# Order of splits, loads and sums around the output projections of a sparse-attention block

## Chip, cores and metric

The kernel runs on one core of a Trainium2 chip. Its time is the device time of one execution in microseconds (us). The engines are TensorE (PE), VectorE (DVE), ScalarE (ACT), GpSimd (POOL) and SyncE (SP); SP, ACT and POOL also issue DMAs, each from its own queue in order.

## The reference, cut to what matters

One block of a decoder trunk: 512 tokens of width 2048, a mixer of native sparse attention (compressed, selected and window branches, 16 heads), then a SwiGLU feed-forward layer of width 5632, then a last normalization. With these sizes only the attention mixer is used.

```python
def rmsnorm(x, g):
    x32 = x.astype(jnp.float32)
    y = x32 * lax.rsqrt(jnp.mean(x32 * x32, axis=-1, keepdims=True) + RMS_EPS)
    return (y * g.astype(jnp.float32)).astype(x.dtype)

def swiglu(h, w_in, w_out):
    z = h @ w_in
    a, b = z[..., :D_FF], z[..., D_FF:]
    return (jax.nn.silu(a) * b) @ w_out

def reference(x, ...):
    h = x
    for i in range(DEPTH):
        hn = rmsnorm(h, mix_norm_g[i])
...
        h = h + nsa_mixer(hn, ...)
...
        h = h + swiglu(rmsnorm(h, ffn_norm_g[i]), ffn_w_in[i], ffn_w_out[i])
    return rmsnorm(h, final_norm_g)
```

## The kernel before

Every matrix product is made of three matmuls in a 32-bit format of lower precision: each operand is split into a high part (an ACT copy into that format) and a low part (a DVE subtraction), and `three` (L275) multiplies high by high, high by low and low by high into the same bank. So every weight costs an ACT and a DVE instruction before PE can use it. `Weights` (L61) loads pieces of 128 x 1024 into three `raw` buffers from SP's queue, splits them into four `whi`/`wlo` buffers, and `take` hands out the next piece, with so many more split ahead. The order of the instructions on each engine is the order in which the code writes them.

**The stages.** The attention mixer comes first (to about 717 us). Along with it the first 1536 columns of the output projection are computed for the first 12 heads, added to `x`, and spilled to `d_h`.

The output projection (L885 to L954) holds the running sum `acc`, four tiles of 128 tokens by 2048 columns. L891 loads columns 1536 on of `x` into it and L892, on POOL's queue, the 1536 spilled columns of all four tiles in one DMA. Then a pass over the last columns, and a loop over tiles `t` and column blocks `cb`: matmuls of the last four heads into one of four banks `po[cb]`, `add` (DVE), a square with a running sum (ACT, L943) whose output goes to a throwaway tile of the four `pp` banks, and for `t` over 0 the transposes of the tile before (`turned`), which need two `pp` banks each. `scaled` applies the norm of the tile, and the finished `acc` rows go to `d_r`.

The first feed-forward product follows (to about 1653 us), in units `q`, with a seven-product scheme for 2 x 2 blocks (Strassen's kind): `split_unit`, `products` and `merge`. Its results go to `d_a`, one slab per pair of inner chunks `j`.

The second product (L1225 to L1433) runs over four column blocks `b` and, in each, 22 units `j` in the order of `ORDER[b]`; `seq` numbers all 88 of them `n`. A unit is either one of seven products (`seven_unit`, 42 matmuls of 256 columns; the inner chunks in `SEVEN[b]`) or plain (`plain_tile` for four token tiles, 24 matmuls of 512 columns). For units of the seven kind the input sums are formed from `d_a` in `form`, and kept in SBUF (`KEPT`, five `asl` slots) or stored in `d_s` and loaded again by `load_seven`, through two `ast` slots. Inputs of plain units, called held, are loaded by `load_a` into one of two places (`rawx`, `tt`) and split by `split_a` into `thi`/`tlo`; `tt` is also where `weight_sums` puts the sums of a seven-kind weight. The residual `acc` is read back from `d_r` by `load_residual` on POOL's queue: columns 0 to 1024 at the start (L1321), the rest as `form` releases the columns that it uses as scratch. At the end of the seven kind's units in a block, `merge_sums` adds the four shared banks `qs` into `acc`; it is written into the next unit, after that unit's splits. `ready` squares a finished block and multiplies it by the last norm's weight.

The last four units of the last block, all plain, form the tail (L1414 to L1435): tile by tile, so that a tile can be finished while the next one is multiplied. A tile's finish is `add`, the square, the multiplication by the weight, `rstd` (sum, mean, root on ACT, and one Newton step on DVE) and four scalings with their stores. `ffn_banks` gives four banks of eight, `po` and `qs` one set each.

Of the kernel before, what the change touches and what calls it, by code (L numbers as in the profile page):

```python
# [10 lines left out]
F32 = mybir.dt.float32  # L11
# [169 lines left out]
def nsa_block(ctx: ExitStack, tc: tile.TileContext, x, rel_bias, mix_g, ffn_g, fin_g, w_in, w_out,  # L181
# [707 lines left out]
    acc = accp.tile([128, NT, D], F32, name="acc")  # L889
    spill = 256 * N_SPILL  # L890
    nc.sync.dma_start(acc[:, :, spill:], x[:, spill:].rearrange("(t p) c -> p t c", p=128))  # L891
    pool.dma_start(acc[:, :, :spill], d_h.rearrange("(t p) c -> p t c", p=128))  # L892

    def add(t, cb, p):
        a = acc[:, t, 512 * cb:512 * (cb + 1)]
        dve.tensor_tensor(a, a, p, op=OP.add)
# [13 lines left out]
    with tc.tile_pool(name="n2", bufs=1) as n2:  # L910
        act(warm, epsc, AF.Sqrt)
        gb2 = n2.tile([128, D], F32, name="gb2")
        pool.dma_start(gb2, ffn_g[0:1, :].to_broadcast([128, D]))
        xn = n2.tile([128, D + 64], F32, name="xn")
        wr_h = n2.tile([128, 7, 1024], F32R, name="wr_h")
        wr_l = n2.tile([128, 7, 1024], F32R, name="wr_l")
        for i in range(7):
            W.place[marks[0] + i] = wr_h[:, i], wr_l[:, i]
        for cb in range(N_SPILL // 2, 4):
            po = out_tiles()  # L920
            for i in range(6):
                w = W.take(2 if cb < 3 else min(2 + i, 6))
                for t in range(NT):
                    tokmajor(po[t], w, heads(i), i == 0, i == 5, t)
            W.ahead(3)
            for t in range(NT):
                add(t, cb, po[t])
        w8 = []
        for t in range(NT):
            ss = smallp.tile([128, 4], F32, name="ss4")  # L930
            po = out_tiles()
            for cb in range(4):
                for i in range(2):
                    if t == 0:
                        w8.append(W.take(7 - len(w8)))
                    tokmajor(po[cb], w8[2 * cb + i], heads(6 + i), i == 0, i == 1, t)
                add(t, cb, po[cb])
                if cb == 3:
                    pool.dma_start(d_r[t], acc[:, t])
                if t and cb in (1, 2):  # L940
                    turned(xn, (2 * cb - 2, 2 * cb - 1), t - 1)
                junk = ps3.tile([128, 512], F32, name="pp")
                act(junk, acc[:, t, 512 * cb:512 * (cb + 1)], AF.Square, accum_out=ss[:, cb:cb + 1])  # L943
            scaled(acc[:, t], rstd(ss), gb2, xn)
            W.ahead((0, 1, 3, 3)[t])
        pa = [ps3.tile([128, 512], F32, name="pp") for _ in range(2)]
        gs = []
        for i in range(4):
            gs.append(W.take(min(2, 3 - i)))
            run(ws(pa, i, gs[i], 0, 256, of=n2_hl))  # L950
            if i in (1, 2):
                turned(xn, (2 * i - 2, 2 * i - 1), 3)
        act(warm, epsc, AF.Silu)
# [152 lines left out]
    def merge(p):  # L1106

        A, B, C, F = banks.pop(p)
        p += N_PLAIN
        e = E[p] = ep.tile([128, 6, 256], F32, name="E")  # L1110

        def both(x):
            return x.unsqueeze(1).to_broadcast([128, 2, 256])

        act(e[:, 1], A[:, 0], AF.Copy)
        plus(e[:, 0:5:4], both(e[:, 1]), B)
        plus(e[:, 5], e[:, 4], F[:, 0])
        plus(e[:, 1], e[:, 5], A[:, 1])
        plus(e[:, 2:4], e[:, 4:6], both(C[:, 0]))
        plus(e[:, 2], e[:, 2], C[:, 1])  # L1120
        if p % 2:
            dve.tensor_tensor(gate_out(p), gate_out(p), gate_out(p - 1), op=OP.mult)
            keep_a(p)
        else:
            act(gate_out(p), gate_out(p), AF.Silu)
# [44 lines left out]


    held, free = {}, {"rawx": -1, "tt": -1}
    for n, (b, j) in enumerate(seq):
        home = "tt"
        if j not in SEVEN[b]:
            home = min(free, key=free.get)
            held[n] = home, free[home]
        free[home] = n

    def load_a(m):  # L1180

        for n, (home, after) in held.items():
            if after == m:
                t = tp.tile([128, 1024 if home == "rawx" else 1536], F32, name=home, bufs=1)
                a_raw[n] = t[:, :2 * S]
                nc.sync.dma_start(a_raw[n], d_a[seq[n][1]])

    def split_a(n):
        if n in held:
            if n >= NU - N_TAIL:  # L1190
                h, l = (asl.tile([128, 1792], F32R, name=f"a{x}")[:, 48:48 + 2 * S] for x in "hl")
            else:
                h, l = (tp.tile([128, 1600], F32R, name=f"t{x}")[:, :2 * S] for x in ("hi", "lo"))
            act(h, a_raw[n], AF.Copy)
            sub(l, a_raw.pop(n), f32(h))
            a_hl[n] = h, l
        elif n < NU:
            a_hl[n] = seven[seq[n][1]] if seq[n][1] in KEPT else passing.pop(0)
        load_a(n)

    t_hl = {}

# [26 lines left out]
    for q in range(NQ):  # L1229
        if q + 1 < NQ:  # L1230
            split_unit(q + 1)
        else:
            W2.ahead(1)
            load_a(-1)
            split_a(0)
        if q + 3 < NQ:
            load_unit(q + 3)
        if q and q % 2 == 0:
            merge(q // 2 - 1)
        products(q)  # L1240
    merge(NQ // 2 - 1)
    front.close()

# [4 lines left out]
    asl = ctx.enter_context(tc.tile_pool(name="asl", bufs=len(KEPT)))  # L1248
    ast = ctx.enter_context(tc.tile_pool(name="ast", bufs=2))
    late2 = ctx.enter_context(tc.tile_pool(name="late2", bufs=1))  # L1250
    ss = [late2.tile([128, 4], F32, name=f"sf{t}") for t in range(NT)]
    n_visit = [0]
    scratch = [acc[:, :, 1024:1536], acc[:, :, 1536:]]
    forms = [n for n, (b, j) in enumerate(seq) if j in SEVEN[b] and (not b or j not in SEVEN[b - 1])]
# [5 lines left out]
    def load_residual(c):  # L1260
        pool.dma_start(acc[:, :, c], d_r[:, :, c].rearrange("t p c -> p t c"))
# [56 lines left out]
            keep_seven(seq[v][1], h, l)  # L1318
            n_visit[0] += 1

    load_residual(slice(0, 1024))  # L1321
    load_form(0)
    load_form(1)
    forming = {n: form(i) for i, n in enumerate(forms)}
# [48 lines left out]
            yield  # L1373

    w8, todo = [], iter(())
    n, na, pending = 0, 1, None
    for b in range(4):
        units = ORDER[b][:-N_TAIL] if b == 3 else ORDER[b]
        po = ffn_banks()
        qs = dict(zip(("p1", "p5", "p6", "p7"), ffn_banks()))  # L1380
        first7 = next(j for j in units if j in SEVEN[b])
        last7 = [j for j in units if j in SEVEN[b]][-1]
        started = False
        for i, j in enumerate(units):
            left = len(units) - 1 - i if b == 3 else 9
            w = W2.take(max(1, 3 - left))
            while na <= n + 1 + max(0, 2 - left):
                split_a(na)
                na += 1
            if pending is not None:  # L1390
                merge_sums(*pending)
                pending = None
            for k in (1, 2, 3, 4):
                next(forming.get(n + k, iter(())), None)
            if j in SEVEN[b]:
                seven_unit(n, w, first7)
            else:
                for t in range(NT):
                    plain_tile(n, w, t, not started, b < 3 and i == len(units) - 1)
            started = True  # L1400
            if j == last7:
                pending = b, qs
            load_seven(n)
            if i >= 4:
                next(todo, None)
            if i == 12:
                gf = late2.tile([128, 512], F32, name="gf")
                nc.sync.dma_start(gf, fin_g[None, 512 * b:512 * (b + 1)].to_broadcast([128, 512]))
            n += 1
        if b < 3:  # L1410
            for t in range(NT):
                add(t, b, po[t])
            todo = ready(b, gf)
    c = slice(1536, 2048)  # L1414
    act(warm, epsc, AF.Sqrt)
    for t in range(NT):
        for i in range(N_TAIL):
            if t == 0:
                w8.append(W2.take(N_TAIL - 1 - i))
                if na < NU:  # L1420
                    split_a(na)
                    na += 1
            plain_tile(n + i, w8[i], t, False, i == N_TAIL - 1)
        add(t, 3, po[t])
        act(po[t], acc[:, t, c], AF.Square, accum_out=ss[t][:, 3:4])
        dve.tensor_tensor(acc[:, t, c], acc[:, t, c], gf, op=OP.mult)
        y = rstd(ss[t])
        for cb in range(4):
            c4 = slice(512 * cb, 512 * (cb + 1))
            src = acc[:, t, c4]  # L1430
            if cb % 2:
                act(src, src, AF.Copy, scale=y)
            else:  # L1433
                dve.tensor_scalar(src, src, y, None, op0=OP.mult)
            (nc.scalar if cb % 2 else nc.sync).dma_start(out[tok(t), c4], src)  # L1435


_INS = ["x", "rel_bias", "mix_norm_g", "ffn_norm_g", "final_norm_g", "nsa_w_in", "nsa_w_out",
# [25 lines left out]
```

## Time and profile before

| | us |
|---|---|
| median of 3 runs | 2132.6 |
| lowest and highest | 2127.05 and 2134.82 |
| the profiled execution | 2126.48 |
| its span in the trace | 2124.5 |
| DVE busy | 1581.9 |
| ACT busy | 998.3 |

In the trace an instruction has its start from the beginning of the span, its duration, its engine, the line of the kernel and the tiles that it writes and reads. A bracket behind it tells how long its engine was idle ahead of it and what it waited for. Matmuls overlap, so that the distance between the starts of two of them says more than their durations. The granted clock is TensorE's, as a share of full speed. PEld is PE's loading of stationary operands; SPq, ACTq and POOLq are the issues of DMAs.

### The profile page before, as it was taken

Reading aid. Unit: us, or ns where it says so; the run is one execution under the profiler, and the core shown is the slowest. Engines: PE = TensorE matmul, PEld = TensorE weight load, DVE = VectorE, ACT = ScalarE, POOL = GpSimd, SP = SyncE. Lnnn points to the kernel's source line nnn. Section 1 sums busy time; section 2 is a strip of 40 time slices with the busy share of each in tenths; the row PEclk is TensorE's granted clock in tenths of the full one; section 3 lists DMA queues with packets and bytes.
Section 4 is the critical chain, followed back from the end, with each engine's and each line's share of the span. In section 5 each row is a group of like instructions: output and inputs, shape, how many; then the busy total and the mean of one; then the engine's idle time right before and its main releaser. Section 6 shows DMA issues by size and latency. Waiting matters only on the chain.

```text
span 2124.5 us, 37555 instructions
## 1 busy us (share of the span) xinstructions
PE 2101.5 (99%) x14831; PEld 1955.1 (92%) x14831; DVE 1581.9 (74%) x2586; ACT 998.3 (47%) x1625; POOL 145.4 (7%) x234
## 2 busy tenths in 40 slices
PE   9999999999999999999999999999999999999997
PEld 7888898888999978999999999999999888999996
DVE  5565667666666366988888888888887778786775
ACT  5344676666655333444343443434433544444444
POOL 2000111111111100000000000000000000000000
PEclk9999999999999999999999999999999999999998
DMA  6655577766796743444343443334333876878784
GB/s 202 187 157 164 157 203 196 194 184 190 225 296 207 233 168 100 137 131 130 120 126 123 130 126 124 121 123 135 120 128 108 312 265 221 320 262 315 272 306 149
DMA packets 257313, 391.26 MB, mean 184 GB/s; under 512 B 27466, under 2 KB 183162, under 8 KB 256496
## 3 DMA queue, kind: packets, MB, share of 16 engines
q1 hardware_dynamic: 227472, 263.64, 39.9%
q0 software_dynamic: 27936, 122.07, 17.1%
q10 hardware_dynamic: 1728, 3.15, 0.4%
q8 instruction: 116, 1.90, 0.4%
q14 instruction: 61, 0.50, 0.1%
HBM read 323.15 MB, written 70.88 MB: 185 GB/s over the span
## 4 chain that ended last, share of the span: by engine, by line
PE 92%; DMA 4%; DVE 2%; ACT 1%; issue 1%; POOL 0%; ACTq 0%; SPq 0%; POOLq 0%; DVEq 0%
PE f L277 14%; PE f L278 13%; PE f L276 13%; PE proj L278 13%; PE proj L276 13%; PE proj L277 13%; PE pp L277 1%; PE pp L278 1%; PE pp L276 1%; DMA pt<-d_p 1%; PE o L277 1%; PE s L276 1%; PE o L278 1%; PE s L278 1%; PE s L277 1%; PE o L276 1%
## 5 line engine op out<-in xcount | busy, mean ns | idle before, releaser
L97 DVE TENSOR_TENSOR wlo<-raw,whi 128x1024 fp32r<-128x1024 f32 (+1 forms) x225 | 270.6, 1206 | 80.6 <-ACT whi L94 80.3
L94 ACT ACTIVATE whi<-raw 128x1024 fp32r<-128x1024 f32 (+1 forms) x225 | 233.2, 1040 | 194.5 <-DVE raw L969 123.5
L276 PE MATMUL proj<-hn_h,whi 128*128 128x512 f32 (+1 forms) x840 | 293.9, 350 | 2.0 <-ACT whi L94 2.0
L278 PE MATMUL proj<-hn_h,wlo 128*128 128x512 f32 (+1 forms) x840 | 291.2, 347 | 0.5 <-DVE wlo L97 0.5
L277 PE MATMUL proj<-hn_l,whi 128*128 128x512 f32 (+1 forms) x840 | 291.0, 346 | 0.0
L969 DVE TENSOR_TENSOR tlo<-tt,thi 128x1536 fp32r<-128x1536 f32 (+2 forms) x134 | 196.0, 1462 | 109.3 <-ACT thi L1071 86.7
L1066 ACT ACTIVATE whi<-raw 128x1024 fp32r<-128x1024 f32 x123 | 126.1, 1058 | 293.7 <-DVE raw L969 290.3
L278 PE MATMUL f<-hn_h,wlo 128*128 128x256 f32 x656 | 181.1, 276 | 0.0
L276 PE MATMUL f<-hn_h,whi 128*128 128x256 f32 x656 | 181.1, 276 | 0.0
L277 PE MATMUL f<-hn_l,whi 128*128 128x256 f32 x656 | 181.1, 276 | 0.0
L278 PEld LDWEIGHTS proj<-hn_h,wlo 128*128 128x128 f32 x840 | 158.1, 188 | 22.5 <-DVE wlo L97 1.2
L276 PEld LDWEIGHTS proj<-hn_h,whi 128*128 128x128 f32 x840 | 158.3, 188 | 19.4 <-ACT whi L94 2.2
L277 PEld LDWEIGHTS proj<-hn_l,whi 128*128 128x128 f32 x840 | 158.1, 188 | 17.2 <-issue 0.2
L276 PE MATMUL proj<-whi,hn_h 128*128 128x256 f32 (+2 forms) x568 | 162.9, 287 | 0.0
L278 PE MATMUL proj<-whi,hn_l 128*128 128x256 f32 (+2 forms) x568 | 162.4, 286 | 0.0
L277 PE MATMUL proj<-wlo,hn_h 128*128 128x256 f32 (+2 forms) x568 | 162.2, 286 | 0.0
L1071 ACT ACTIVATE thi<-tt 128x1536 fp32r<-128x1536 f32 x82 | 121.8, 1486 | 82.6 <-PE proj L277 82.5
L969 DVE TENSOR_TENSOR wlo<-raw,whi 128x1024 fp32r<-128x1024 f32 x123 | 147.0, 1223 | 1.1 <-ACT whi L1066 1.1
L277 PEld LDWEIGHTS f<-hn_l,whi 128*128 128x128 f32 x656 | 123.2, 188 | 0.0
L276 PEld LDWEIGHTS f<-hn_h,whi 128*128 128x128 f32 x656 | 123.1, 188 | 0.0
L278 PEld LDWEIGHTS f<-hn_h,wlo 128*128 128x128 f32 x656 | 123.1, 188 | 0.0
L760 ACT ACTIVATE p<-p,ms 128x31 f32<-128x31 f32 (+2 forms) x192 | 90.6, 473 | 43.4 <-DVE ms L758 40.6
(346 smaller groups left out, 6232.2 us busy)
## 6 DMA issues: line engine op xcount, KB each, us to landing
raw<-in_ffn_w_in SPq DMA_DIRECT2D x135, 512.0 KB, 3.7
raw<-in_ffn_w_out SPq DMA_DIRECT2D x88, 512.0 KB, 5.8
rawx<-in_ffn_w_in SPq DMA_DIRECT2D x41, 512.0 KB, 4.8
rawx<-d_a SPq DMA_DIRECT2D x34, 512.0 KB, 4.9
ah<-d_s POOLq DMA_DIRECT2D x16, 896.0 KB, 6.9
al<-d_s POOLq DMA_DIRECT2D x16, 896.0 KB, 9.2
raw<-in_nsa_w_in SPq DMA_DIRECT2D x24, 512.0 KB, 4.9
raw<-in_nsa_w_in POOLq DMA_DIRECT2D x24, 512.0 KB, 6.1
```

The costliest lines, as they stand in the source:

```text
L94: self.nc.scalar.activation(hi[:, :n], src, AF.Copy)
L97: self.nc.vector.tensor_tensor(lo[:, :n], src, hi[:, :n].bitcast(F32), op=OP.subtract)
L276: mm(o, ah, bh, start=start, stop=False, skip_group_check=True)
L277: mm(o, ah, bl, start=False, stop=False, skip_group_check=True)
L278: mm(o, al, bh, start=False, stop=stop, skip_group_check=True)
L760: act(p, p, AF.Exp, bias=s["mx"][:, t, i:i + 1], scale=-1.0, accum_out=s["sm"][:, t, i:i + 1])
L969: dve.tensor_tensor(o, a, b, op=OP.subtract)
L1066: act(h, r, AF.Copy)
L1071: act(h, ttf, AF.Copy)
```

## The change

- The spilled sums are loaded by token tile: the first on POOL's queue at the old place, the others on SP's queue in the loop over tiles.
- The squares in that loop write over the bank that was just added, not over a `pp` bank.
- The splits of unit 1's input and weight are written ahead of the last `merge` of the first product.
- The residual's columns 0 to 1024 are loaded in two blocks, at unit 9 of block 0 and unit 6 of block 1.
- The tail's four inputs are no longer held: `load_tail` loads each into the low part of an `asl` slot that its chunk has left, and `split_tail` splits it there, during the last block. `rawx` and `tt` lose these loads.
- The last block's `merge_sums` is written behind the matmuls of the tail's first tile.
- A tile's finish is new: the sum of the first three blocks' squares is made ready ahead (`known`), ACT takes the root right from the last square's sum, the Newton step is written with two reciprocals (`factor`), and the weight's multiplication goes into the scaling (`send`).
- The tail's last tile is multiplied in halves of 256 columns, the second half into the bank of `qs["p7"]`, and each half is added and squared by itself (`last_columns`).

```diff
-    pool.dma_start(acc[:, :, :spill], d_h.rearrange("(t p) c -> p t c", p=128))
+    def load_sum(t, eng=nc.sync):
+        eng.dma_start(acc[:, t, :spill], d_h[tok(t)])
+
+    load_sum(0, pool)
...
                 add(t, cb, po[cb])
+                if (t, cb) in ((0, 1), (0, 3), (1, 1)):
+                    load_sum(2 * t + cb // 2 + 1)
...
-                junk = ps3.tile([128, 512], F32, name="pp")
-                act(junk, acc[:, t, 512 * cb:512 * (cb + 1)], AF.Square, accum_out=ss[:, cb:cb + 1])
+                act(po[cb], acc[:, t, 512 * cb:512 * (cb + 1)], AF.Square, accum_out=ss[:, cb:cb + 1])
...
-    for n, (b, j) in enumerate(seq):
+    for n, (b, j) in enumerate(seq[:-N_TAIL]):
...
+    def load_tail(i):
+        n = NU - N_TAIL + i
+        a_hl[n] = [asl.tile([128, 1792], F32R, name=f"a{x}")[:, 48:48 + 2 * S] for x in "hl"]
+        nc.sync.dma_start(f32(a_hl[n][1]), d_a[seq[n][1]])
+
+    def split_tail(i):
+        h, l = a_hl[NU - N_TAIL + i]
+        act(h, f32(l), AF.Copy)
+        sub(l, f32(l), f32(h))
...
         products(q)
+    split_a(1)
+    W2.split()
     merge(NQ // 2 - 1)
...
-    load_residual(slice(0, 1024))
...
-            if pending is not None:
+            if pending is not None and pending[0] < 3:
                 merge_sums(*pending)
                 pending = None
+            if b == 3 and i in (4, 8, 12, 15):
+                load_tail((i - 3) // 4)
+            if b == 3 and i in (7, 11, 14, 17):
+                split_tail((i - 6) // 4 + (i == 17))
...
+            if (b, i) in ((0, 9), (1, 6)):
+                load_residual(slice(512 * b, 512 * (b + 1)))
...
+    def last_columns(t, o, c0, c1, j):
+
+        a = acc[:, t, 1536 + c0:1536 + c1]
+        dve.tensor_tensor(a, a, o, op=OP.add)
+        act(o, a, AF.Square, accum_out=ss[t][:, j:j + 1])
+
+    def known(t, j):
+
+        p = smallp.tile([128, 1], F32, name="ms")
+        dve.tensor_reduce(p, ss[t][:, :j], axis=AX.X, op=OP.add)
+        dve.tensor_scalar(p, p, q4, 0.25 * EPS, op0=OP.mult, op1=OP.add)
+        return p
+
+    def factor(t, j, p):
...
+        z = ss[t][:, j:j + 1]
+        act(s, z, AF.Sqrt, scale=q4, bias=p)
+        dve.scalar_tensor_tensor(a, z, q4, p, op0=OP.mult, op1=OP.add)
+        dve.reciprocal(y, s)
+        dve.scalar_tensor_tensor(a, a, y, s, op0=OP.mult, op1=OP.add)
+        dve.reciprocal(y, a)
+        return y
+
+    def send(t, y, on_act):
+        for cb in (3, 1, 0, 2):
+            src = acc[:, t, 512 * cb:512 * (cb + 1)]
+            if cb == 3:
+                dve.scalar_tensor_tensor(src, src, y, gf, op0=OP.mult, op1=OP.mult)
+            elif cb in on_act:
+                act(src, src, AF.Copy, scale=y)
+            else:
+                dve.tensor_scalar(src, src, y, None, op0=OP.mult)
+            eng = nc.scalar if cb == 2 and cb in on_act else nc.sync
+            eng.dma_start(out[tok(t), 512 * cb:512 * (cb + 1)], src)
...
+        if not t:
+            merge_sums(*pending)
+            a = acc[:, NT - 1, 1792:]
+            dve.tensor_tensor(a, a, po[NT - 1][:, 256:], op=OP.add)
+        p = known(t, 3)
+        last_columns(t, po[t], 0, 512, 3)
+        send(t, factor(t, 3, p), (1,))
+    t = NT - 1
+    ends = po[t][:, :256], qs["p7"][:, :256]
+    for u, o in enumerate(ends):
+        for i in range(N_TAIL):
+            for k in range(2):
+                ah, al = (x[:, S * k:S * (k + 1)][:, tok(t)] for x in a_hl[n + i])
+                three(o, ah, al, *(x[:, k, 256 * u:256 * (u + 1)] for x in w8[i]), u == 1 and i == 0 and k == 0,
+                      i == N_TAIL - 1 and k == 1)
+    last_columns(t, ends[0], 0, 256, 3)
+    p = known(t, 4)
+    last_columns(t, ends[1], 256, 512, 4)
+    send(t, factor(t, 4, p), (1, 2))
```

More of the change, by code (lines that the diff above doesn't have):

```diff
@@ L1189, in split_a @@
         if n in held:
[L1190 to L1193, printed above, removed]
+            h, l = (tp.tile([128, 1600], F32R, name=f"t{x}")[:, :2 * S] for x in ("hi", "lo"))
             act(h, a_raw[n], AF.Copy)
@@ L1196, in split_a @@
             a_hl[n] = h, l
-        elif n < NU:
+        elif n < NU - N_TAIL:
             a_hl[n] = seven[seq[n][1]] if seq[n][1] in KEPT else passing.pop(0)
         load_a(n)
+    def load_tail(i):
[6 more added lines that the diff above has]
+        sub(l, f32(l), f32(h))
     t_hl = {}
@@ L1250, in nsa_block @@
     late2 = ctx.enter_context(tc.tile_pool(name="late2", bufs=1))
-    ss = [late2.tile([128, 4], F32, name=f"sf{t}") for t in range(NT)]
+    ss = [late2.tile([128, 4 + t // 3], F32, name=f"sf{t}") for t in range(NT)]
     n_visit = [0]
@@ L1375, in nsa_block @@
     w8, todo = [], iter(())
-    n, na, pending = 0, 1, None
+    n, na, pending = 0, 2, None
     for b in range(4):
@@ L1413, in nsa_block @@
             todo = ready(b, gf)
-    c = slice(1536, 2048)
     act(warm, epsc, AF.Sqrt)
-    for t in range(NT):
+    q4 = 0.25 / D
+    def last_columns(t, o, c0, c1, j):
[8 more added lines that the diff above has]
+    def factor(t, j, p):
+        a, y = (smallp.tile([128, 1], F32, name=x) for x in ("nt", "rs"))
+        s = late2.tile([128, 1], F32, name="root")
+        z = ss[t][:, j:j + 1]
[16 more added lines that the diff above has]
+            eng.dma_start(out[tok(t), 512 * cb:512 * (cb + 1)], src)
+    for t in range(NT - 1):
         for i in range(N_TAIL):
@@ L1419, in nsa_block @@
                 w8.append(W2.take(N_TAIL - 1 - i))
-                if na < NU:
-                    split_a(na)
-                    na += 1
             plain_tile(n + i, w8[i], t, False, i == N_TAIL - 1)
[L1424 to L1435, printed above, removed]
+        if not t:
[17 more added lines that the diff above has]
+    send(t, factor(t, 4, p), (1, 2))
 _INS = ["x", "rel_bias", "mix_norm_g", "ffn_norm_g", "final_norm_g", "nsa_w_in", "nsa_w_out",
```

## The prediction

> **What bounds the kernel now.** I read the page first, for the busiest engine and the chain that ended last, then stages of the span, then the timelines where TensorE (PE) idles.
>
> ```profile
> span 2124.5 us, 37555 instructions
> ...
> PE 2101.5 (99%) x14831; PEld 1955.1 (92%) x14831; DVE 1581.9 (74%) x2586; ACT 998.3 (47%) x1625; POOL 145.4 (7%) x234
> ...
> PE 92%; DMA 4%; DVE 2%; ACT 1%; issue 1%; POOL 0%; ACTq 0%; SPq 0%; POOLq 0%; DVEq 0%
> ```
>
> PE bounds it, and the change takes no matmul column away. So it can win only where PE waits, where its clock is low, and behind the last matmul. The view by stages finds these places (columns: stage, its length, busy time of PE, weight loads, DVE, ACT, POOL, then the granted clock, DMA share, GB/s):
>
> ```profile
> 751.00:754.00 3.00, 0.97 (x5) 0.54 (x4) 3.00 (x4) 1.95 (x2) 0.00 (x0) 1.00 0.35 100
> ...
> 1661.00:2089.00 428.00, 427.91 (x2795) 389.64 (x2794) 334.87 (x480) 196.48 (x238) 27.04 (x50) 1.00 0.80 283
> 2089.00:2094.00 5.00, 1.84 (x7) 0.91 (x5) 4.90 (x6) 0.80 (x1) 0.00 (x0) 0.98 0.00 0
> 2094.00:2101.00 7.00, 6.41 (x17) 5.03 (x17) 3.60 (x11) 1.64 (x4) 0.00 (x0) 0.52 0.01 2
> ```
>
> The long stage, 428 us, holds 0.1 us of idleness. PE waits near 751, 800, 1659 and 2089, and after the last wait its clock is at 0.52.
>
> **The change part by part.**
>
> *Spilled sums by token tile.* In the timeline:
>
> ```profile
> 732.34 0.75 POOL L892 DMA_DIRECT2D acc<-d_h  x1 [9.27 <-DMA d_h<-stage]
> ...
> 749.67 2.22 ACT L94 ACTIVATE wr_h<-raw 128x1024 fp32r<-128x1024 f32 x2 [4.24 <-DMA raw<-in_nsa_w_out]
> ...
> 751.43 0.39 PE L278 MATMUL po<-whi,hn_l 128*128 128x512 f32 x1
> 753.85 0.47 PE L276 MATMUL proj<-wr_h,hn_h 128*128 128x512 f32 x1 [2.03 <-ACT wr_h L94]
> ```
>
> and among the DMA issues (count, size, us to landing):
>
> ```profile
> acc<-d_h POOLq DMA_DIRECT2D x1, 3072.0 KB, 13.9
> ...
> ah<-d_s POOLq DMA_DIRECT2D x16, 896.0 KB, 6.9
> ```
>
> The 3 MB load runs beside the weight loads; ACT waits 4.24 us for a weight piece, DVE's low parts and then `add`, which frees the bank, follow in order, and PE starts 2.42 us after its last matmul where the step is 0.23. Now 768 KB goes first. At 3 MB in 13.9 us the other 2.3 MB held about 10 us of DMA; without them these pieces land earlier by more than the 2.2 us lacking. Gain **2.2** (bounds 0 and 2.2). The other three loads stand on SP behind the third `in_ffn_w_in` load, which is issued during tile 0; tile 1's first add comes a tile later, 48 matmuls of 0.23 = 11 us, and a transfer of 896 KB takes 6.9. A late one holds up `add`, and PE only when the bank comes round, another tile later: taken as nothing.
>
> *Squares over their own banks.* `turned` shares four `pp` banks with the junk of the squares:
>
> ```profile
> 799.25 0.39 PE L278 MATMUL po<-wr_h,hn_l 128*128 128x512 f32 x1
> 799.94 0.66 PE L254 MATMUL pp<-ident,xn 128*128 128x128 f32 x4 [0.30 <-ACT pp L943]
> 801.15 0.66 PE L254 MATMUL pp<-ident,xn 128*128 128x128 f32 x4 [0.55 <-DVE hn_l L265]
> 801.56 0.48 PE L276 MATMUL po<-wr_h,hn_h 128*128 128x512 f32 x1
> ```
>
> Four transposes take 0.41 (801.15 to 801.56); the stretch from 799.25 should be 0.23 + 0.82 = 1.05 and is 2.31. Without junk, eight buffer turns per tile become four, and neither wait is left: **1.3** (bounds 0 and 1.3). New: PE waits for the square, not the add, before it writes a bank again; that is a tile later, so free.
>
> *Unit 1 split ahead of the last merge.*
>
> ```profile
> 1653.47 0.38 ACT L1115 ACTIVATE E<-proj 128x256 f32<-128x256 f32 x1 [3.09 <-PE proj L278]
> ...
> 1655.14 0.42 DVE L972 TENSOR_TENSOR E<-E,proj 128x256 f32<-128x256 f32 x1
> ...
> 1658.92 1.22 DVE L969 TENSOR_TENSOR tlo<-tt,thi 128x1024 fp32r<-128x1024 f32 x1
> ...
> 1659.06 0.49 PE L277 MATMUL proj<-wlo,thi 128*128 128x512 f32 x1
> 1660.20 0.50 PE L278 MATMUL proj<-whi,tlo 128*128 128x512 f32 x1 [0.64 <-DVE tlo L969]
> ```
>
> PE loses about 1.0 because tlo stands behind the merge. But DVE works without a break from 1653.9 on, so its work is only reordered; and the earlier split waits for the `thi` slot that the last product holds until 1653.5, then ACT, so DVE starts about 0.7 later (1654.6). Unit 1 is then in time, unit 2 nearly, and what unit 3 needs comes 0.7 later to a PE that is 1.0 earlier. I take **0.3** (0 to 1.0). The merge itself moves 3 us back; its banks are used again three units later.
>
> *Residual by blocks.* The 2 MB at the start become 1 MB at unit 9 and 1 MB at unit 28 on POOL's queue. By the condition in `load_seven` no `d_s` load follows them for several units, the blocks' first users come ten or more units later, and PE has no wait there to win: 0; its price if cover fails is the fourth rival.
>
> *Last tiles and root.* The timeline at the end of the matmuls:
>
> ```profile
> 2085.80 0.39 PE L276 MATMUL proj<-whi,ah 128*128 128x512 f32 x1
> ...
> 2087.07 0.68 DVE L972 TENSOR_TENSOR m<-m,f 128x512 f32<-128x512 f32 x1
> ...
> 2089.88 0.47 PE L276 MATMUL proj<-whi,ah 128*128 128x512 f32 x1
> ...
> 2092.24 1.22 DVE L97 TENSOR_TENSOR wlo<-raw,whi 128x1024 fp32r<-128x1024 f32 x1
> 2093.37 1.22 DVE L969 TENSOR_TENSOR al<-rawx,ah 128x1024 fp32r<-128x1024 f32 x1
> 2093.51 0.54 PE L277 MATMUL proj<-wlo,ah 128*128 128x512 f32 x1 [3.16 <-DVE wlo L97]
> ```
>
> From 2085.80 to 2089.88 are 18 matmuls, 0.227 each. Then the last piece's wlo and al come behind 5.2 us of `merge_sums` on DVE (2087.07 to 2092.24). PE has its next start at 2093.51 and the one after at about 2094.65, when al is done (2093.37 + 1.22): 4.77 for two steps of 0.23, so **4.3** lost. With the inputs loaded into free `asl` slots and split units earlier, and the merge behind the last weight split, wlo is ready by 2085.8 + 1.1 + 1.2 = 2088.1 (it waits for unit 17 to leave its buffer) and is needed at 2090.1. The clock's price: in the chain of waits the steps are 0.43 instead of 0.23,
>
> ```profile
> 2095.44 0.43 PE proj L276
> ...
> 2100.14 0.43 PE f L278
> ```
>
> 12 such steps from the first of these rows to the last, 0.20 extra in each, and 0.4 in the slow ones beside them: **2.8**. SP's new wait, `load_tail` for PE to leave a slot, has weight loads queued behind it; the slots' last users lie one or two units back, as far as the weight loads' own waits reach: 0.
>
> The Trainium skill, "TensorE: Matmul & The Clock Gate", Part 1, says that the clock halves after an idle window of 3413 ns, and that the windows run free of the kernel. The 0.98 and 0.52 above agree, as does the 1.00 at the shorter wait of 751. By that rule the 2.8 would be lost only in runs whose window falls into the wait; that is the second rival.
>
> Halves of the last tile cost no PE time by the spacing of 256-column matmuls: these are 23 steps,
>
> ```profile
> 2072.17 0.28 PE L276 MATMUL proj<-whi,ah 128*128 128x256 f32 x1
> ...
> 2074.78 0.28 PE L278 MATMUL f<-whi,al 128*128 128x256 f32 x1
> ```
>
> 0.1135 each, half of 0.227. Behind the last matmul:
>
> ```profile
> 2114.56 0.39 PE L278 MATMUL f<-whi,al 128*128 128x512 f32 x1
> ...
> 2114.99 0.69 DVE L896 TENSOR_TENSOR acc<-acc,f 128x512 f32<-128x512 f32 x1 [1.02 <-PE f L278]
> 2115.71 0.60 ACT L1425 ACTIVATE f<-acc 128x512 f32<-128x512 f32 x1 [0.76 <-DVE acc L896]
> ...
> 2117.44 0.20 ACT L228 ACTIVATE rs<-ms 128x1 f32<-128x1 f32 x1 [1.01 <-DVE ms L227]
> ...
> 2118.51 0.88 DVE L1434 TENSOR_SCALAR acc<-acc,rs 128x512 f32<-128x512 f32 x2
> ...
> 2120.40 0.34 ACTq L1435 DMA_DIRECT2D out<-acc  x1
> ```
>
> Add and square on 256 columns: 0.42 for 0.69, about 0.38 for 0.60: 0.5 less. The root starts on ACT right behind the accumulator instead of 1.01 later: 0.9 less. Root to factor: three small steps for four, 0.2 less. No DMA issue (0.35) between ACT's two last copies: 0.35 less. Together **1.95**. From this goes 0.2: the merge (2088.2 to 2093.4) now delays tile 0's end on DVE. A tile's chain is then 0.37 + 0.72 + 0.75 (square) + 0.25 (root) + 0.7 + 1.5 (three scalings) = 4.3 us against PE's 5.44, so from 2093.8 tile 2 is through at 2106.7, and the final add starts near 2108.0 instead of 2107.8. Left **1.75**.
>
> Sum: 2.2 + 1.3 + 0.3 + 4.3 + 2.8 + 1.75 = 12.65, say **12.7 us**. The profiled execution took 2126.5 (span 2124.5 and 2 around it): 2113.8. It lies 6.1 under the median of the three runs, 2132.6, for no reason that the trace shows; from the median the forecast is **2119.9**.
>
> **The rivals.**
>
> 1. *DVE's new queue at the end.* For: the chain of 4.3 is made of estimates, and 2.9 us of backlog stand before it. From 5.4 us per tile on nothing is made up, and 2.9 come back at the end: 2122.8. Against: the removed multiply and four small steps made up the old chain, which kept pace.
> 2. *The half clock is not in the usual run.* For: the wait of 2.03 us at 753.85 left the clock at 1.00 and the one of 3.16 at 2093.51 did not; the limit lies between, and one trace is all there is. Then 2.8 fall out of the gain: 2122.7.
> 3. *The change doesn't do it*: the last weights still come late, since their buffer is free only when unit 17 ends, or a load of `asl` slots stalls SP. The margin is 2.0 us. Then 7.1 stay: 2127.
> 4. *Slower*: the two 1 MB residual loads at units 9 and 28 run beside the `d_s` stores and delay weights. Price: a late landing and, if PE idles long enough, 2.8 of half clock. For it:
>
> ```profile
> acc<-d_r POOLq DMA_DIRECT2D x2, 1024.0 KB, 10.5
> ```
>
> so 2 x (10.5 + 2.8) = 26.6: 2146.5 (that would be 0.65% slower). It decides once a weight piece, asked for three units (15 us) ahead, is over 10 us late. Against it: `form` already puts a 1 MB residual load between `d_s` stores and loads, in the middle of this stage, and all that PE's side waits for a `d_s` load in the whole of it is
>
> ```profile
> PEld f L278 <- DMA al<-d_s: 0.3, 1, 0.3
> ```
>
> **How the numbers follow.** Forecast 0.58, rivals 0.14, 0.18, 0.05 and 0.05. A run of this kernel can tell about 0.5% from no change: 10.7 us, 2121.9. Forecast is beyond it; rivals 1 to 3 are within. So faster 0.58, same 0.37, slower 0.05. Best sum: 1.0 for the 0.3 gives 2119.2, and the lowest of the three runs is 5.6 under the median: 2113.5. The high end takes in rivals 1 and 2 and just reaches 3: 2127. Out of it stay rival 4, half of 3 and some scatter, under 0.2.
>
> **What would show it.** Right: no PE wait over 0.5 us behind the first 20 us, clock 1.00 until the last matmul, last matmul to last DMA issue about 4.0 instead of 5.8. Wrong: a wait on a weight piece, `tlo` or `al` near units 2 and 3 or at the last piece, a final add much over 0.6 behind the start of its matmul, a wait on DMA near units 9 and 28; and the whole forecast if a median doesn't move as the profiled execution does.

## The result and the profile after

| | before | after |
|---|---|---|
| median of six runs each, us | 2130.21 | 2116.87 |
| lowest and highest | 2126.18 and 2134.82 | 2114.17 and 2118.46 |
| the profiled execution | 2126.48 | 2114.17 |

The time is 0.994 of that before, with a 95% interval of 0.9926 to 0.9953: 13.3 us less by the medians, 12.3 by the profiled executions. The forecast was 12.7. The page of the changed kernel, its span, busy times and the chain that ended last:

```profile
span 2112.3 us, 37622 instructions
...
PE 2099.1 (99%) x14855; PEld 1955.7 (93%) x14855; DVE 1581.2 (75%) x2587; ACT 996.4 (47%) x1624; POOL 145.5 (7%) x235
...
PE 97%; DVE 1%; DMA 1%; ACT 0%; issue 0%; SPq 0%; DVEq 0%; ACTq 0%
```

PE's own share of that chain went from 92% to 97%: what went was waiting, not work. PE has 24 matmuls more, since the last tile's 24 became 48 of half the width. Its view by stages has the same columns as before:

```profile
12.00:30.00 18.00, 17.47 (x75) 12.53 (x74) 10.01 (x28) 11.19 (x19) 5.47 (x10) 0.81 0.76 246
751.00:754.00 3.00, 3.00 (x14) 2.46 (x14) 1.84 (x3) 1.06 (x1) 0.00 (x0) 1.00 0.54 185
1661.00:2089.00 428.00, 427.47 (x2794) 389.27 (x2793) 336.85 (x482) 195.67 (x236) 28.46 (x52) 1.00 0.79 282
2089.00:2094.00 5.00, 5.00 (x23) 4.14 (x23) 3.80 (x12) 1.75 (x4) 0.00 (x0) 1.00 0.00 0
2094.00:2101.00 7.00, 7.00 (x43) 6.22 (x42) 4.84 (x18) 2.77 (x7) 0.00 (x0) 1.00 0.76 277
```

PE is busy all through 751 to 754 and 2089 to 2101, and the clock of 0.52 in the last of these stages is now 1.00. The long stage got 0.5 us of idleness. The first line is a stretch in which both kernels run the same instructions. In the trace of before it reads

```profile
12.00:30.00 18.00, 17.47 (x83) 13.11 (x82) 11.23 (x30) 12.76 (x21) 5.49 (x10) 0.91 0.83 264
```

so this execution of the changed kernel began at a lower clock, 0.81 for 0.91, and lost 1.6 us there, which has nothing to do with the change; smaller differences in the rest of the mixer leave 0.99 of it in the ledger below. PE's longest wait behind the first 20 us (us in total, times, longest):

```profile
PE f L278 <- DVE al L974: 0.5, 1, 0.5
```

It is new. The trace of before has none there.

**The ledger.** I read off the starts of the same matmuls in both traces and so cut the span into stretches: the output projection from its first matmul into `po` to the first into `pp` of the feed-forward product; the second product from its first matmul to the tail's first; the tail to the last matmul; and what follows.

| stretch | before | after | difference | forecast |
|---|---|---|---|---|
| start to output projection | 721.74 | 722.73 | +0.99 | 0 |
| output projection | 82.66 | 78.80 | -3.86 | -3.5 |
| first feed-forward product | 848.87 | 848.87 | 0 | 0 |
| second product up to the tail | 432.53 | 431.62 | -0.91 | -0.3 |
| tail | 28.76 | 21.95 | -6.81 | -7.1 |
| last matmul to last DMA issue | 5.84 | 3.97 | -1.87 | -1.75 |
| issue to the end | 4.06 | 4.35 | +0.29 | 0 |

The sum is -12.17, the difference of the ends (2124.46 and 2112.29, where the last instruction of each trace starts). These stretches are what the experiments below go by, because the time of one execution scatters by more than any single part of this change is worth. (Some expectations take a neighbouring matmul as first of the tail; by the count used here their 431.4 is 431.6, and their 22.2 and 29.0 are 21.95 and 28.76.)

**Output projection.** The timeline of the changed kernel: DVE's low parts of the weights `wr` and its first `add`, PE around the first use of `wr`, then PE at the last transposes:

```profile
746.05 2.54 DVE L97 TENSOR_TENSOR wr_l<-raw,wr_h 128x1024 fp32r<-128x1024 f32 x2 [0.17 <-ACT wr_h L94]
748.77 0.69 DVE L900 TENSOR_TENSOR acc<-acc,proj 128x512 f32<-128x512 f32 x1 [0.18 <-PE proj L278]
...
752.42 0.39 PE L278 MATMUL po<-whi,hn_l 128*128 128x512 f32 x1
752.65 0.39 PE L276 MATMUL proj<-wr_h,hn_h 128*128 128x512 f32 x1
...
797.69 0.39 PE L278 MATMUL po<-wr_h,hn_l 128*128 128x512 f32 x1
797.92 1.03 PE L254 MATMUL pp<-ident,xn 128*128 128x128 f32 x8
```

What PE needs at 752.65 is the bank `proj`, which the first `add` frees. On DVE that `add` stands behind the low parts of six weight pieces. They are through by 748.59 now, `add` follows PE at 748.77, and PE goes on after a plain step of 0.23. In the trace of before the same `add` came behind the late pieces:

```profile
753.07 1.28 DVE L896 TENSOR_TENSOR acc<-acc,proj 128x512 f32<-128x512 f32 x2
```

The first of these two `add`s was done at about 753.75, and PE started at 753.85. (The bracket of that wait names a copy of the weights, but that copy had ended 0.66 us earlier, and PE's other waits in that trace end within 0.14 us of what they waited for.) The eight transposes of a half tile run as one group, with no bracket. The loads of sums and residual among the DMA issues:

```profile
acc<-d_r POOLq DMA_DIRECT2D x4, 1024.0 KB, 11.2
...
acc<-d_h SPq DMA_DIRECT2D x3, 768.0 KB, 7.4
```

**Second product.** Its beginning, on DVE and PE:

```profile
1651.62 1.23 DVE L974 TENSOR_TENSOR tlo<-tt,thi 128x1024 fp32r<-128x1024 f32 x1 [2.87 <-ACT thi L1196]
...
1666.41 1.22 DVE L974 TENSOR_TENSOR al<-acc,ah 128x1024 fp32r<-128x1024 f32 x1
...
1667.69 0.38 PE L278 MATMUL f<-thi,al 128*128 128x256 f32 x1 [0.53 <-DVE al L974]
```

Unit 1's `tlo` starts 1.2 us after the first matmul of the second product (1651.62), where it was 5.6 (1658.92), and PE's wait is gone. At unit 3, DVE is behind by the merge that it put off, and PE waits for `al`.

**Tail and end.**

```profile
2083.31 1.23 DVE L97 TENSOR_TENSOR wlo<-raw,whi 128x1024 fp32r<-128x1024 f32 x1 [3.47 <-ACT whi L94]
2084.45 0.68 DVE L977 TENSOR_TENSOR m<-m,f 128x512 f32<-128x512 f32 x1
...
2086.10 0.39 PE L276 MATMUL proj<-whi,ah 128*128 128x512 f32 x1
...
2094.31 0.15 DVE L1445 TENSOR_REDUCE ms<-sf 128x1 f32<-128x3 f32 x1
...
2098.47 0.15 DVE L1445 TENSOR_REDUCE ms<-sf 128x1 f32<-128x3 f32 x1
...
2103.97 0.28 PE L278 MATMUL f<-whi,al 128*128 128x256 f32 x1
2104.29 0.42 DVE L1439 TENSOR_TENSOR acc<-acc,f 128x256 f32<-128x256 f32 x1 [0.31 <-PE f L278]
...
2105.28 0.29 ACT L1454 ACTIVATE root<-sf,ms 128x1 f32<-128x1 f32 x1
...
2107.04 1.30 SPq L1471 DMA_DIRECT2D out<-acc  x3
```

The last weight's low part is done at 2084.5; the fourth unit, which needs it, starts at 2086.10 and uses it from its second matmul on. The merge starts only behind it. DVE needs 4.16 us per tile (2094.31 to 2098.47) against PE's 5.44. So DVE stands idle when the last matmul ends (the bracket of 0.31), and the add comes 0.32 behind that matmul's start. The root starts 0.99 behind the add, and the last DMA, the third of that group on SP's queue, is issued 2.66 behind the root, at 2107.94.

### The profile page after: what moved, and what is told of

The parts are those of the page before. It is cut to its first block, busy times and chain, and to the rows that moved or that the text cites. A ratio compares the mean times of both kernels' runs of the same rounds, so it can differ in the third digit from the quotient of the medians.

```text
span 2112.3 us, 37622 instructions
## 1 busy us (share of the span) xinstructions
PE 2099.1 (99%) x14855; PEld 1955.7 (93%) x14855; DVE 1581.2 (75%) x2587; ACT 996.4 (47%) x1624; POOL 145.5 (7%) x235
## 4 chain that ended last, share of the span: by engine, by line
PE 97%; DVE 1%; DMA 1%; ACT 0%; issue 0%; SPq 0%; DVEq 0%; ACTq 0%
PE proj L276 14%; PE proj L278 14%; PE proj L277 14%; PE f L277 14%; PE f L278 14%; PE f L276 14%; PE pp L277 1%; PE pp L278 1%; PE pp L276 1%; PE o L277 1%; PE o L278 1%; PE s L276 1%; PE o L276 1%; PE s L278 1%; PE s L277 1%; DMA pt<-d_p 1%
```

## The experiments

Each kernel is the changed one with one edit; the diffs are against it. Each ran once beside a run of the kernel before on the same chip, except the last, for which the medians of four and seven executions stand. Columns: time, that of the kernel before beside it, and four of the stretches (output projection, second product, tail, last matmul to last DMA issue).

| kernel | us | before | output pr. | second pr. | tail | to issue |
|---|---|---|---|---|---|---|
| the change | | | 78.80 | 431.62 | 21.95 | 3.97 |
| one load of sums | 2118.45 | 2130.68 | 81.24 | 432.06 | 21.95 | 3.97 |
| throwaway squares | 2115.12 | 2130.68 | 80.35 | 431.32 | 21.95 | 3.97 |
| late split | 2113.69 | 2130.68 | 78.80 | 431.63 | 21.95 | 3.97 |
| merge in its old place | 2112.65 | 2130.68 | 78.80 | 431.38 | 22.03 | 3.97 |
| late inputs | 2119.00 | 2126.86 | 78.80 | 431.83 | 23.03 | 5.37 |
| whole last tile | 2116.11 | 2126.86 | 78.80 | 433.03 | 21.53 | 4.56 |
| old root | 2115.27 | 2126.86 | 78.80 | 431.39 | 21.95 | 7.06 |
| residual at the start | 2114.93 | 2131.13 | 78.80 | 432.21 | 21.95 | 3.97 |
| tail inputs at column 0 | 2119.35 | 2126.86 | 78.80 | 431.78 | 22.34 | 3.97 |
| tail inputs at four columns | 2115.35 | 2131.13 | 78.80 | 432.24 | 22.27 | 3.97 |
| a product on POOL | 2115.24 | 2131.13 | 78.80 | 432.35 | 21.95 | 3.97 |
| other order in unit 3 | 2116.96 | 2128.63 | 78.80 | 432.30 | 21.95 | 3.97 |

The output projection and the tail come out equal to 0.01 us wherever they were not touched. The second product does not: in kernels that leave it as the change has it, it lies between 431.32 and 432.24, and at 433.03 in one execution, which has a wait of 1.01 near 1711, far from its edit. A difference of under 0.9 there says nothing by itself.

**One load of the spilled sums.**

```diff
-    load_sum(0, pool)
+    pool.dma_start(acc[:, :, :spill], d_h.rearrange("(t p) c -> p t c", p=128))
...
-                if (t, cb) in ((0, 1), (0, 3), (1, 1)):
-                    load_sum(2 * t + cb // 2 + 1)
```

> The changed kernel, but with all spilled sums in one 3 MB load at the old place. The stretch from the output projection's first po<-whi matmul to the first pp<-hn_h,whi matmul is 78.8 us in the changed kernel (722.73 to 801.52) and 82.7 before. Theory, the 3 MB load delays weight pieces and these the adds: PE waits about 2 us again ahead of its first wr_h matmul, stretch 81.0. Rival, the weights come late for another reason (the load of gb, chance of one run): wait under 0.5, stretch 79 or less.

The output projection became 2.44 longer, nearly all of it at one place of its timeline; that transfer's row among the DMA issues stands below it:

```profile
755.51 1.28 DVE L900 TENSOR_TENSOR acc<-acc,proj 128x512 f32<-128x512 f32 x2
756.29 0.47 PE L276 MATMUL proj<-wr_h,hn_h 128*128 128x512 f32 x1 [2.16 <-ACT wr_h L94]
```

```profile
acc<-d_h POOLq DMA_DIRECT2D x1, 3072.0 KB, 13.9
```

The wait is back with the large transfer and with nothing else, and again PE starts 0.1 us after the first `add` is done. So it was the transfer that held up the weights, and through their low parts on DVE the `add`.

**Squares into a throwaway bank.**

```diff
-                act(po[cb], acc[:, t, 512 * cb:512 * (cb + 1)], AF.Square, accum_out=ss[:, cb:cb + 1])
+                junk = ps3.tile([128, 512], F32, name="pp")
+                act(junk, acc[:, t, 512 * cb:512 * (cb + 1)], AF.Square, accum_out=ss[:, cb:cb + 1])
```

> The changed kernel, but with the squares written to a throwaway pp tile. Theory, the squares' share of the four pp banks makes the transposes wait: the two waits of about 0.3 and 0.6 us at tile 3's second pair of transposes return, the stretch from the first po<-whi matmul to the first pp<-hn_h,whi matmul grows from 78.8 to 80.1 (1.3), or to 80.5 if the 0.4 that this stretch won beyond the forecast came from the banks too. Rival, the waits were those of a DVE made late by the 753.85 wait and were gone without the banks: under 79.2.

Longer by 1.55, and both waits of the trace of before are back:

```profile
798.33 0.66 PE L254 MATMUL pp<-ident,xn 128*128 128x128 f32 x4 [0.33 <-ACT pp L949]
...
799.54 0.66 PE L254 MATMUL pp<-ident,xn 128*128 128x128 f32 x4 [0.55 <-DVE hn_l L265]
```

The square, as the second user of the four banks, causes both, the one put down to `hn_l` too.

**Unit 1 split behind the merge, as before.**

```diff
-    split_a(1)
-    W2.split()
     merge(NQ // 2 - 1)
...
-    n, na, pending = 0, 2, None
+    n, na, pending = 0, 1, None
```

> The changed kernel, but with unit 1's splits behind the last merge again. From the second product's first matmul to the tail's first is 431.4 us in the changed kernel, 432.3 before. Theory, DVE's work is the same and only its order changes: the wait of about 0.9 at unit 1 returns, the one of 0.7 at unit 3 goes, 431.4 + 0.3 = 431.7. Rival, the early splits are worth the whole wait and unit 3's comes from something else: 431.4 + 1.0 = 432.4 with unit 3's wait still there.

The wait at unit 1 is back, and that at unit 3 is gone:

```profile
1656.84 0.50 PE L278 MATMUL proj<-whi,tlo 128*128 128x512 f32 x1 [0.63 <-DVE tlo L974]
```

The stretch is 431.63, as with the change. The early split moves a wait of the same size from unit 1 to unit 3. What it is worth lies below the scatter of this stretch; counted from the first matmul of the second product, PE's lead with the change grows to 1.1 at unit 1 and falls back to 0.3 at unit 3, over this kernel as over the kernel before.

**The merge in its old place, the inputs early.**

```diff
-            if pending is not None and pending[0] < 3:
+            if pending is not None:
...
-            merge_sums(*pending)
             a = acc[:, NT - 1, 1792:]
```

> The changed kernel, with its early inputs of the tail, but with the last block's merge_sums in the old place, ahead of the tail. The tail's first matmul to its last takes 22.2 us in the changed kernel and 29.0 before. Theory, the merge was late only because the inputs that came late stood ahead of it on DVE: with early inputs it runs in time, no PE wait over 0.5, no half clock, 22.2 to 22.6. Rival, the merge itself in that place is what costs: a PE wait on wlo of 2 us or more, 24.5 or more.

No wait in the tail, which is 22.03 long. With the inputs split early, the merge's move wins nothing.

**The inputs late, the merge behind the first tile.** The tail's inputs go through `rawx` and `tt` again, and `load_tail` and `split_tail` are gone.

```diff
-    for n, (b, j) in enumerate(seq[:-N_TAIL]):
+    for n, (b, j) in enumerate(seq):
...
-        elif n < NU - N_TAIL:
+        elif n < NU:
...
                 w8.append(W2.take(N_TAIL - 1 - i))
+                if na < NU:
+                    split_a(na)
+                    na += 1
```

> The changed kernel, with the merge behind the tail's first tile, but with the tail's inputs loaded through rawx and tt and split late, as before. Tail, first matmul to last: 22.2 us in the changed kernel, 29.0 before. Theory, late inputs and the merge behind them add up on DVE, and the merge's 5.2 us are the larger part: without it the last al comes about 0.8 us late, no half clock, 23.0. Rival, the late inputs alone are the cause: a wait of 3 us or more and the half clock, 27 or more.

The tail is 23.03, about as expected, but 1.40 is lost behind it. PE at the fourth unit, the start of the merge and then the end of the timeline:

```profile
2089.71 0.68 DVE L977 TENSOR_TENSOR m<-m,f 128x512 f32<-128x512 f32 x1
2089.85 0.50 PE L278 MATMUL proj<-whi,al 128*128 128x512 f32 x1 [0.53 <-DVE al L974]
...
2107.43 0.28 PE L278 MATMUL f<-whi,al 128*128 128x256 f32 x1
2107.90 0.41 DVE L1438 TENSOR_TENSOR acc<-acc,f 128x256 f32<-128x256 f32 x1
...
2109.15 0.41 DVE L1438 TENSOR_TENSOR acc<-acc,f 128x256 f32<-128x256 f32 x1
```

PE's wait is short, and the clock stays at 1.00 behind it. But the merge starts 5.3 us later than with the change (2089.71 for 2084.45), and the tail 2.4 later (2084.39 for 2082.02), so that DVE is 2.9 behind PE, and it has not made up for that when the last matmul starts at 2107.43: the first half's add starts only at 2107.90, the last at 2109.15, 1.72 behind its matmul. This is the first rival of the prediction, in a kernel where its condition holds. So of the two moves the early inputs do it all, and the merge's move alone takes 5.7 off the tail and gives 1.4 back at the end.

**The last tile whole.**

```diff
-    for t in range(NT - 1):
+    for t in range(NT):
...
-    ends = po[t][:, :256], qs["p7"][:, :256]
...
-    last_columns(t, ends[0], 0, 256, 3)
...
+        send(t, factor(t, 3, p), (1,) if t < NT - 1 else (1, 2))
```

> The changed kernel, but with the last tile multiplied whole, in 24 matmuls of 512 columns. In the changed kernel the halves' 48 matmuls step at 0.118 us where the seven-product units step at 0.1135, and from the start of the last matmul to the last DMA issue are 3.97 us. Theory: PE's part of the last tile gets 0.2 shorter, last matmul to last issue 0.5 to 0.6 longer (add 0.69 for 0.42, square 0.60 for 0.39, a longer last matmul), in sum 0.3 to 0.4 later. Rival, the halves only move the work and DVE's queue ends both alike: within 0.1.

The tail is 0.42 shorter and what follows 0.59 longer: the halves are worth 0.2. The end of its timeline:

```profile
2105.33 0.39 PE L278 MATMUL f<-whi,al 128*128 128x512 f32 x1
2105.76 0.69 DVE L1439 TENSOR_TENSOR acc<-acc,f 128x512 f32<-128x512 f32 x1 [1.18 <-PE f L278]
```

The add takes 0.69 for 0.42 and all of it stands behind the last matmul.

**The old root and scalings, the halves kept.**

```diff
-        p = known(t, 3)
         last_columns(t, po[t], 0, 512, 3)
-        send(t, factor(t, 3, p), (1,))
+        send(t)
...
+        dve.tensor_tensor(acc[:, t, c], acc[:, t, c], gf, op=OP.mult)
+        y = rstd(ss[t])
...
+            (nc.scalar if cb % 2 else nc.sync).dma_start(out[tok(t), c4], src)
```

> The changed kernel, halves too, but with the old finish of a tile (sum, mean, root, four small steps, weight multiplied ahead, two scalings each on ACT and DVE with ACT's own stores). Last matmul to last DMA issue: 3.97 us in the changed kernel, 5.84 before. Theory: halves give 0.5 of the 1.9, the root behind the square and the fewer steps the rest: 5.3. Rival, the halves give nearly all: 4.3 or less.

Neither account has it: 7.06, though 0.5 of that comes back behind the last issue (3.86 us to the end for 4.35). The timeline shows why:

```profile
2103.18 0.75 DVE L1438 TENSOR_TENSOR acc<-acc,f 128x256 f32<-128x256 f32 x2
2103.52 0.72 ACT L1449 ACTIVATE acc<-acc,rs 128x512 f32<-128x512 f32 x1 [0.42 <-ACT acc L1449]
2104.27 0.34 ACTq L1452 DMA_DIRECT2D out<-acc  x1
2104.66 0.39 ACT L1439 ACTIVATE f<-acc 128x256 f32<-128x256 f32 x1 [0.41 <-ACT acc L1449]
...
2105.60 0.69 DVE L1443 TENSOR_TENSOR acc<-acc,gf 128x512 f32<-128x512 f32 x1 [1.67 <-ACT f L1439]
...
2109.54 0.34 ACTq L1452 DMA_DIRECT2D out<-acc  x1
```

The two last adds are one pair from 2103.18 on, so the first half did not go ahead. The square, at 2104.66, stands on ACT behind the tile before: its second copy at 2103.52 and a store's issue. DVE waits 1.67 for it. With the old finish the merge behind the first tile does leave a backlog to the end: DVE's `add`s of the second and third tile start 5.12 us apart here, against 4.16 with the new finish and 5.44 of PE. So the new finish shortens the end, and it also lets DVE make up for that place of the merge.

**The residual at the start, as before.**

```diff
-            if (b, i) in ((0, 9), (1, 6)):
-                load_residual(slice(512 * b, 512 * (b + 1)))
...
+    load_residual(slice(0, 1024))
```

> The changed kernel, but with the residual's columns 0 to 1024 loaded at the start of the second product in one 2 MB DMA, as before. The second product takes 431.4 to 431.6 us in the changed kernel, with PE waits of 0.7 at unit 3 and about 0.1 at 1709. Theory, the place of these loads is worth nothing as PE's weights are asked for far enough ahead: 431.3 to 431.9, the same waits. Rival, the blocks' loads delay weights at units 9 and 28, or the 2 MB load delays the first units: waits of 0.5 or more that the changed kernel doesn't have, or the other way.

PE's waits in the second product are now two, the second in unit 4:

```profile
PE f L278 <- DVE al L974: 0.6, 1, 0.6
PE proj L278 <- DVE tlo L974: 0.5, 1, 0.5
```

The stretch is 0.59 longer, which one execution cannot tell from its scatter. The blocks cost nothing, and may be worth a few tenths.

**Where the tail's inputs lie in their slots.** The first kernel puts them at column 0, the second at columns 8, 16, 32 and 40 for the four units.

```diff
-[:, 48:48 + 2 * S]
+[:, 0:0 + 2 * S]
```

```diff
-[:, 48:48 + 2 * S]
+[:, (8, 16, 32, 40)[i]:(8, 16, 32, 40)[i] + 2 * S]
```

> The changed kernel, but with the tail's inputs at column 0 of their asl slots, not 48. The last tile's 48 matmuls of 256 columns step at 0.118 to 0.120 us there, and at 0.113 to 0.115 in the seven-product units. Theory, the step depends on where the stationary operand lies in memory against the moving one: 0.113 to 0.116 at column 0, 0.2 us less in all. Rival, it comes from other work beside the last tile (DVE, ACT, stores): 0.118 to 0.120 again.

> The changed kernel, but with the four tail inputs at columns 8, 16, 32 and 40 of their asl slots, one each. At column 48 the matmuls of 512 columns step at 0.227 us and those of 256 at 0.120; at column 0 at 0.235 and 0.118. Theory, the step hangs on the stationary operand's place against the moving one: the four inputs show different steps, between 0.216 and 0.235 for 512 columns. Rival, column 0 differed by its slots or by chance: all four at 0.227 and 0.120.

The mean step of the tail's matmuls depends on the column, though not as I expected: 512 columns take 0.227 at 48, but 0.233 at 0, and 0.233, 0.233, 0.230 and 0.233 at 8, 16, 32 and 40. Those of 256 take 0.120 at 48 and 0.118 at 0, where the seven-product units have 0.1135. The tail comes out 0.39 and 0.32 longer, so column 48 stays the best of those tried for this tail. The two kernels have one trace each, and why the place matters is open.

**The last gate product on POOL**, to free DVE for 1.23 us ahead of unit 3.

```diff
-            dve.tensor_tensor(gate_out(p), gate_out(p), gate_out(p - 1), op=OP.mult)
+            (pool if p == NF - 1 else dve).tensor_tensor(gate_out(p), gate_out(p), gate_out(p - 1), op=OP.mult)
```

> The changed kernel, but with the last product of the first layer (gate times value, 1.23 us on DVE, the end of the last merge) on POOL instead of DVE. Theory, unit 3's wait of 0.7 is DVE's work after 1651 us in one piece, so 1.1 less of it takes the wait away: second product 430.7 to 430.9 instead of 431.4 to 431.6. Rival, something else in that chain (the form's loads, ACT) ends as late, or POOL slows DVE: wait of 0.4 or more still there.

The rival held. The timeline:

```profile
1657.07 2.47 POOL L1127 TENSOR_TENSOR E<-E 128x1024 f32<-128x1024 f32 x1 [36.30 <-DVE E L977]
1657.18 2.63 DVE L974 TENSOR_TENSOR acc<-acc 128x256 f32<-128x256 f32 x1
```

The subtraction on DVE that starts beside POOL's product takes 2.63 us; the two that follow it take 0.4 each, and so do all three with the change. DVE gives 1.23 away and loses 2.2, and PE waits 0.6 us twice, for `tlo` and for `al`.

**Another order of products in unit 3**, so that its first products don't need the late `al`.

```diff
+        order = ("p1", "p5", "p2", "p3", "p7", "p6", "p4") if n == 3 else ("p7", "p6", "p1", "p5", "p2", "p3", "p4")
+        for name in order:
```

> The changed kernel, but unit 3, the first of the seven-product kind, begins with p1, p5, p2 and p3, which need neither the sums of weights nor the last third of its input sums, and only then takes p7, p6 and p4. Theory, its wait of 0.7 is for these two alone, and 24 matmuls of 0.1135 = 2.7 us ahead of them cover it: no wait of 0.5 between 1651 and 1680, second product 430.7 to 430.9 instead of 431.3 to 431.6. Rival, DVE's work comes as late to unit 4, as with the 2 MB load at the start: a wait of 0.5 or more there, and 431.3 or more. Time against the kernel before: as the changed kernel, 0.994.

Between 1651 and 1680 PE no longer waits, but this execution has waits of 0.41 near 1711 and 1878, and the stretch is 432.30. The median over rounds is 2116.96, 0.994 of the kernel before (0.992 to 0.9961): no better than the change.

## Why the prediction was right, step by step

The forecast of 2119.9 stood on the three runs shown, whose median of 2132.6 lies 2.4 above that of six runs. Its gain of 12.7 lies between the 12.3 and 13.3 measured. The terms:

- **Spilled sums: 2.2 forecast, 2.2 in the ledger, 2.44 in the experiment.** Right in mechanism and size.
- **Squares: 1.3 forecast, 1.67 in the ledger with small waits around it, 1.55 in the experiment.** The estimate counted the last group of transposes only; the kernel before waits a little in the tiles ahead too.
- **Unit 1: 0.3.** Right, and near nothing: the wait of 0.64 moves to unit 3, which the prediction had named as late, and is 0.53 there; PE's lead behind it is 0.3. This wait on `al` is also the one of the prediction's signs of being wrong that came. The other 0.6 that the second product gained is not explained by any part; it lies within that stretch's scatter.
- **Residual: 0.** Nothing was lost at units 9 and 28, where no wait stands. The fourth rival falls.
- **Tail: 4.3 and 2.8 forecast, together 7.1, 6.81 measured.** With a whole last tile the tail is 21.53, which is 7.23 less than before: waits and clock were worth 0.1 more than forecast. The term mis-sized is the one taken as free, halves at "0.1135 each". In this tail the steps are 0.120, and the halves take 0.42 of the 7.23 back: 48 times 0.0065 is 0.3, and the rest comes of counting to the start of a last matmul that is half as long.
- **End: 1.75 forecast, 1.58 measured.** Up to the last issue 1.87 is gained, and 0.29 of it is lost again until the end; the likely reason is that the last two stores are now issued 0.31 apart, where it was 0.95. Of the 1.95 counted, the halves gave 0.59 (forecast 0.5, and paid for by the 0.42 that they cost in the tail), and the new finish with a whole tile 5.84 - 4.56 = 1.28 (forecast 1.45). The 0.2 taken off for DVE's backlog was not needed: the add comes 0.32 behind its matmul, not 0.6.

The reason given for the tail holds more than was needed. The prediction credits early inputs and late merge together. The experiments show that early inputs suffice, and that the merge's move would run into the first rival without them.

**The rivals.** The first needs a merge that starts late. In the late-inputs kernel its price was 1.4, about half of the 2.9 given. The third (weights late in any case) falls by 1.8 us: `wlo` was done at 2084.5 and needed at 2086.3, where 2.0 were forecast. The second is not settled by measurement: only one execution of the kernel before has a trace. Two things speak against it. Had the 2.8 us been lost in the profiled execution alone, the usual gain would be 12.3 - 2.8 = 9.5; the interval of the ratio is 10.0 to 15.8 us. And by the steps of the clock in the last section, the waits of 3.16 and 0.59 us in the tail put at least 1.88 us of idleness into one step wherever the steps fall, and over the 1.93 that was always followed by half clock in 96% of the positions. How long the half clock then lasts, one step or two, and so whether it costs the whole 2.8 each time, stays open.

That the profiled execution, forecast at 2113.8, came out at 2114.17 is partly luck: the mixer took 1 us more, and the second product and the transposes gave as much more than was counted.

## What to carry to other kernels

Where one engine is busy 99% of the time, list its few waits by stage and ask of each which small piece stands behind which large one in a queue: a 3 MB load ahead of a 512 KB weight, a throwaway output in a bank that another step needs, 5 us of sums ahead of the last split. Splitting by first use, or preparing the inputs earlier, then takes the whole wait, while a mere reordering on an engine that has no slack (unit 1 here) moves it a few units on. When work is pushed towards the end of a kernel, check that each later stage leaves the engine time to catch up, and what happens where it doesn't.

## What was not expected of the hardware

**The clock after a wait does not go by its length alone.** In the mixer, near 610 us, PE waits for `pth` for a time that varies from one execution to the next: not at all with the change, 0.45 before, 2.15 in the late-inputs kernel, whose timeline and stage there read

```profile
610.56 0.44 PE L276 MATMUL o<-pth,v1h 128*128 128x384 f32 x1 [2.15 <-ACT pth L799]
```

```profile
608.64:612.05 3.41, 1.34 (x7) 1.09 (x8) 1.51 (x8) 2.07 (x5) 0.00 (x0) 1.00 1.07 243
612.05:615.47 3.42, 3.42 (x18) 3.42 (x17) 3.23 (x7) 3.42 (x10) 0.00 (x0) 0.50 0.43 145
```

Behind 2.15 us of waiting the clock was at half for 3.4 us, while it stayed at 1.00 behind 2.16 with one load of sums and behind 2.03 before, where the stage around the wait reads

```profile
752.40:755.81 3.41, 1.96 (x9) 1.65 (x10) 3.41 (x6) 0.79 (x1) 0.00 (x0) 1.00 0.73 208
```

So it matters when a wait falls as well as how long it is. The clock records of the fourteen traces show how: each spell of one clock between two changes lasts a whole number of steps of 3.413 us (3.41, 6.83, 10.24, 593.92, 2088.96 and so on). The stages above are laid on these steps. The wait near 610 leaves 3.41 - 1.34 = 2.07 us of one step idle; the wait of 2.03 leaves 1.45; that of 2.16 is cut in two, 1.16 and 1.00. Behind the first 20 us of all the traces, half clock follows every step with 1.93 us of idleness or more, and none with 1.85 or less; in the first 20 us it also came after less, and why is open. The Trainium skill, "TensorE: Matmul & The Clock Gate", Part 1, has windows of 3413 ns that run free of the kernel, which fits the dependence on the moment and the length of the drop; that a whole idle window is needed does not fit, since 1.93 us of one was enough here, and the wait of 3.16 in the tail of before left 3.09 idle of the step that it fell into.

**The start-up clock and that wait make most of the scatter between traces.** The stage from 12 to 30 us had 0.91, 0.81 and 0.72 in different executions, and the wait near 610 went up to 3.3 us. The stretch up to the output projection, which no edit touches, took 721.4 to 727.4 us: a range larger than most parts of this change are worth.

**A product on POOL holds up a subtraction on DVE beside it** (2.63 us for 0.42, while the product takes 2.47). The Trainium skill, "SBUF — State Buffer", under "Who interferes with whom", says that a DVE instruction with two inputs from SBUF contends with a GpSimd instruction that reads SBUF; the trace agrees.

**A matmul's step depends on the place of its operand in SBUF**, by up to 3% at 512 columns (0.227 to 0.233).
